# A list scheduler's prices for TensorE operations are replaced in a two-layer transformer block

## The chip, the cores and the metric

The kernel runs on one core of a Trainium2 chip. The metric is the device time of one execution in microseconds, the median of the timed runs.

## The reference

Two layers of a diffusion transformer work on 256 latent tokens and 256 context tokens of width 1024, all in 32-bit floats. In short:

```python
for l in range(2):
    mod_l = silu(c) @ w_ada[l] + b_ada[l]                # six rows: shift, scale, gate, twice
    h = x * (1 + sc1) + sh1                              # the context likewise, with its own rows
    ya, yb, yc, yd = four attentions of one projection h @ w_in[l]
    #   latent, neighbourhood, differential, grouped-query; 4 heads each
    #   latents read latents and context, the context reads context only
    out = (sum_i sigmoid(gate_i) * (y_i @ w_branch[l, i])) @ w_out[l]
    x = layer_norm(ALPHA * x + g1 * out)
    h = x * (1 + sc2) + sh2
    x = layer_norm(ALPHA * x + g2 * (silu(h @ w_gate) * (h @ w_up)) @ w_down[l])
return x                                                 # the latents
```

The context stream stops after the attentions' keys and values of the second layer, so that layer's queries, gates and FFN cover 256 tokens instead of 512.

## The kernel before

Every matrix product is made of three: both operands are split into a high and a low part on the reduced 32-bit grid of TensorE, and high*high, high*low and low*high are added in one PSUM bank (`mm3`). A weight tile of 128x1024 arrives by one DMA of 512 KB into `wr`; ScalarE casts it to the high part `wh`, VectorE subtracts for the low part `wl`. In the first layer most products have a moving operand of 512 columns, in the second of 256. The activations are `hh` and `hl`, those of the FFN `fh` and `fl`; `mm`, `st` and `o` are the PSUM tiles of projections, of scores and transposes, and of attention outputs.

In neighbourhood and grouped-query attention a score is two products (`scores2`, line 865): one over 128 rows and one over 64 rows, `k,q` 128 and `gt,q` or `l,q` or `k,q` 64 in the profile. The 128-row operand holds a head's parts in both halves of the partitions, so `heads2` (line 853) moves them there by DMAs from SBUF to SBUF:

```python
        self.split(a, lo, ps[:, :n], scale)
        self.move(b[64:, :], a[64:, :])
        self.move(b[:64, :], (lo if q else a)[64:, :])
        self.move(a[64:, :], (lo if q else a)[:64, :])     # after both others have read a
```

The order of the instructions is not written by hand. The kernel is recorded on virtual tiles; `record` (line 249) gives each operation a price in microseconds from `price` (line 280), and a list scheduler orders the instructions of each engine. `schedule` (line 313) runs up to ten passes (`PASSES`, line 227). `forward` (line 382) simulates the engines forward in time; an engine takes, among the operations that are ready by then, the one with the smallest priority number:

```python
            lim = t + LOOK[e]                              # LOOK: 0.03 us for TensorE
            op = min((o for o in ready[e] if o.est <= lim), key=lambda o: (o.prio, o.idx))
            op.start = max(t, op.est)
            free[e] = op.start + op.cost
            if e == "sync":                                # a DMA; dge is 0.65 between SBUF tiles
                dge_free = max(op.end, dge_free) + op.dge
                dma_free = max(dge_free + 0.65, dma_free) + op.bytes / 360e3
                op.end = dma_free + 0.95
```

`backward` (line 333) then goes the same way backwards and makes new priorities of the latest starts; the pass with the shortest simulated length is kept. The tables `SEE` and `SEE_OTHER` hold what passes until one engine sees another's result. Which of a tag's buffers a tile gets is decided by the same passes. `emit` issues everything in the order found, each engine runs its own list in that order, and the waits follow from the data. Because every instruction is issued from one place, all rows of the profile name line 535; the tiles tell them apart.

The prices of the other engines: a ScalarE operation 0.05 or 0.09 + 0.833e-3 per element and 0.093 per pointer operand, a VectorE tensor_tensor 0.065 + n / 960, a DMA 0.05 on its queue.

Of the kernel before, what the change touches and what calls it, by code (L numbers as in the profile page):

```python
# [31 lines left out]
# columns of the per-layer column array  # L32
# [8 lines left out]
# ---------------------------------------------------------------------------  # L41
# Order of issue.  The kernel is recorded on virtual tiles; a list scheduler
# over its dependences then orders the instructions of each engine, and Tile
# gets them in that order (it allocates the tiles and adds every wait).
# ---------------------------------------------------------------------------
# [26 lines left out]
class View:  # L72
    """A view of a virtual tile: shape and strides (in elements) and the calls that make it."""
# [61 lines left out]
    def region(self):  # L135
        """Partitions and the runs of elements in them."""
        row = self.tile.row
        p0 = self.off // row
        p1 = p0 + (self.shape[0] - 1) * (1 if self.strides[0] else 0) + 1
        runs, width = [self.off % row], 1  # L140
        for n, st in sorted(zip(self.shape[1:], self.strides[1:]), key=lambda x: x[1]):
            if st <= width or n == 1 or len(runs) * n > 16:
                width += (n - 1) * st
            else:
                runs = [r + i * st for i in range(n) for r in runs]
        return p0, p1, tuple((r, min(r + width, row)) for r in sorted(runs))
# [36 lines left out]
class Slot:  # L183
    """The i-th memory of a tag's tiles; after: the slots of later phases that lie on it."""
# [34 lines left out]
# time until an engine sees what another has written (its own: what it wrote itself), in us  # L219
# [6 lines left out]
# passes of the scheduler, and how far an engine looks ahead for something more urgent, in us  # L226
# [5 lines left out]
class Plan:  # L232
# [47 lines left out]
    def price(self, op, ins, outs):  # L280
        """Time on the engine, in us."""
        eng, kw = op.eng, op.kw
        if eng == "tensor":
            if op.meth == "transpose":
                n = kw["in_"].shape[0]
                return max(64, n) * 2.1 / 2400
            n = max(64, kw["rhs"].free())
            return n / 2400 + 0.0026 if kw["rhs"].dtype == F32R else n * 4 / 2400 + 0.43
# [24 lines left out]
    def schedule(self):  # L313
        """Forward passes, by program order at first, then by the latest starts that the last pass allows."""
        for op in self.ops:
            for p in op.preds:
                p.succs.append(op)
        best = None
        for _ in range(PASSES):
            order = self.forward()  # L320
            if order is None:
                break
            if best is None or self.length < best[0]:
                best = self.length, order, [o.start for o in order], [(t, t.slot.i) for o in order for t in o.tiles]
            self.backward(order)
        self.length, order, starts, places = best
        for t, i in places:
            t.place = i
        for o, t in zip(order, starts):
            o.start = t  # L330
        return order

    def backward(self, order):
        """The same backwards in time: the order of each engine by latest starts."""
# [47 lines left out]
    def forward(self):  # L382
# [12 lines left out]
        # slots of a tag go to its tiles in the order in which the kernel makes them  # L395
# [64 lines left out]
        while done < len(ops):  # L460
# [30 lines left out]
            for tl in op.tiles:  # L491
                if tl.pool.psum:
                    # no two engines at once on a bank
                    for o in tl.users:
                        if o.eng != e:
                            o.est = max(o.est, op.end + SEE[e].get(o.eng, SEE_OTHER[e]))
# [41 lines left out]
class Net:  # L538
# [14 lines left out]
    # ---------------------------------------------------------------- helpers  # L553
# [9 lines left out]
    def w_tile(self, kind, dtype):  # L563
        """Weight tiles go round the slots of the common pool and, in part, of the phase's own."""
# [15 lines left out]
    def load_w(self, src, n, gain=None, dst=None):  # L580
        """Some weights, split; gain: per-partition factors of equal runs of the columns."""
# [22 lines left out]
    def split(self, hi, lo, src, scale=None):  # L604
        """hi + lo == src, both on the 32-bit reduced grid of the tensor engine."""
# [8 lines left out]
    def blk(self, wh, wl, c0, c1, ps=None):  # L614
        """One block of 128 output features, transposed: [features, tokens c0:c1]."""
# [10 lines left out]
    # ------------------------------------------------------------------ setup  # L626
# [15 lines left out]
    def condition(self, pool):  # L642
        """silu of the conditioning vectors, on all partitions."""
# [12 lines left out]
    # -------------------------------------------------------------- modulation  # L656
    def ada_plan(self, items):
        """Modulation columns to compute, (layer, block, streams) each, handed out by ada_step."""
# [19 lines left out]
    def affine(self, l, m_sh, m_sc, s, lnl=None, lnw=0):  # L678
        """Per-feature scale and shift of the next sublayer's input, [128, 8] each."""
# [16 lines left out]
    def first_h(self):  # L696
        """Shift and scale of the first sublayer by the tensor engine, for some features at a time: rows
        [high and low parts of 2, shift | scale], then columns; behind them the first input itself."""
# [64 lines left out]
    def early(self, q):  # L763
        """The weights by which the first blocks take up one part of the features."""
# [23 lines left out]
    def modulate(self, parts, hi, lo, pool, a):  # L788
        """x * G + B for two pieces of 256 columns, split."""
# [11 lines left out]
    def bc_rows(self, l, m, s, scale, pool):  # L801
        """Row m of the modulation as two [128, 512] tiles, the same on all partitions, by way of DRAM."""
# [13 lines left out]
    # ------------------------------------------------------------- projections  # L816
    def proj_b(self, src, w, per, toks, evac, cols=None):
        """[tokens, w] for each token tile; src(kts) gives the weights of some k tiles."""
# [27 lines left out]
    def qk(self, tag, rows=P):  # L846
        """Two tiles over the queries or the keys, in one."""
# [5 lines left out]
    def heads2(self, ps, q, lo, scale=None):  # L853
        """Two heads of 64 rows, for scores in two products: queries [qh; ql] and [ql; qh], or keys [kh; kh]
        twice, with the low parts of the keys left in lo."""
# [31 lines left out]
    def transposed(self, srcs, rows, cols_of):  # L887
        """[rows, tokens] from token-major tiles, in one bank."""
# [5 lines left out]
    # --------------------------------------------------------------- attention  # L894
    def softmax(self, S, n, scale, rs):
        """exp(scale * (S - max)) and its sum, by rows."""
# [26 lines left out]
    def head(self, s, prob, V, vh, yrow, ydst):  # L923
        """Output of one head on one stream: prob(qt) gives [128 queries, keys]."""
# [33 lines left out]
    def pow_cols(self, ss, n, a, b, tag="rms", bufs=8):  # L958
        """(a * ss + b) ** -0.5"""
# [6 lines left out]
    # neighbourhood attention  # L966
    def na_proj(self, l):
# [11 lines left out]
        for b in range(4):  # L979
            if b == 2 and l:  # L980
                # latents first: their gates need no context
# [38 lines left out]
    # latent attention  # L1020
# [111 lines left out]
    def rope_b(self, v, t, nh, dim, C, S):  # L1132
        """In place on v [128 tokens, nh, dim], tables [128, dim]."""
# [14 lines left out]
    # differential attention  # L1148
# [17 lines left out]
    def df_block(self, l, b, t):  # L1166
        """Queries or keys of two heads, rotated and split."""
# [17 lines left out]
    def df_stack(self, i, q, k, last):  # L1185
        """The three products of a score in one: [qh; qh; ql] against [kh; kl; kh]."""
# [26 lines left out]
    def df_attn(self, l, st, lam_init):  # L1213
# [6 lines left out]
        for c in range(2):  # L1220
            for i in range(2):
                h = 2 * c + i
                sq, sk = qk[h]
                for s in self.streams:
                    def prob(qt):
# [8 lines left out]
                        # (lam e2 / s2) s1 - e1: minus s1 times the difference; the norm takes s1 out  # L1234
# [10 lines left out]
        for t in self.qtoks:  # L1245
# [9 lines left out]
            # (ss / 64 + EPS * s1 ** 2) ** -0.5  # L1255
# [18 lines left out]
    # grouped-query attention  # L1274
# [83 lines left out]
    # ------------------------------------------------------------ gated merge  # L1358
# [6 lines left out]
    def fill(self, n):  # L1365
        """Some steps of work that what comes next does not need."""
# [41 lines left out]
    # ----------------------------------------------------- projection, residual  # L1408
# [3 lines left out]
    def f_pair(self, j):  # L1412
        """1024 columns of the FFN's activation tiles, from block j on."""
# [3 lines left out]
    def residual(self, ps, bc, x, t, half, st, c0=0, c1=512):  # L1417
        """x <- alpha * x + mod * ps, some columns of a token tile, and their statistics."""
# [14 lines left out]
    def out_proj(self, l, t, bc, xs):  # L1433
        """One token tile through w_out, the residual and the norm."""
# [14 lines left out]
    def down_proj(self, l, bc, xs, held, apply, after):  # L1449
        """w_down by halves of 512 features; the last pieces with the tokens outside."""  # L1450
# [7 lines left out]
        for half in range(2):  # L1458
            # the last token tile of all ends by quarters
# [31 lines left out]
    def next_h(self, s, x, aff, pool, kps=range(4)):  # L1491
        """From the normalised x: the modulated, transposed and split input of the next sublayer."""
# [12 lines left out]
    def next_ht(self, t, x, aff, pool):  # L1505
        """The same for one token tile of the latents."""
# [11 lines left out]
    def affine_x(self, x, l, w, tile):  # L1518
        """x * g + b of a norm, by halves of the features."""
# [10 lines left out]
    # ------------------------------------------------------------------- layer  # L1530
# [77 lines left out]
    def ffn_lead_both(self, l, xs, pool, bc, aff):  # L1608
        """w_out, norm and the first FFN blocks, latents in front of the context."""
# [14 lines left out]
    def ffn_lead_lat(self, l, xs, pool, bc, aff):  # L1624
        """w_out, norm and the first four FFN blocks by token tiles."""
# [32 lines left out]
    def ffn(self, l, xs, pool, last, bc, aff):  # L1658
# [18 lines left out]
        if not last:  # L1677
            self.aff1 = aff = {s: self.affine(l + 1, 0, 1, s, l, 1) for s in self.streams}

            def after(t):  # L1680
                # the last two k tiles hold weights that the context still needs
# [46 lines left out]
def _ktile(w, n0, n1):  # L1728
    """[L, K, N] columns n0:n1 -> [L, 128, (K/128) * (n1-n0)]"""
# [5 lines left out]
def _blocks(w):  # L1735
    """[L, K, N] -> [L, N/128, 128, K] with row p of block b holding w[k*128+p, b*128:...] for all k"""
# [4 lines left out]
def _layout(i):  # L1741
# [44 lines left out]
    # neighbourhood bias: rpb[h, i - r + 7, j - w + 15] inside the window, NEG outside  # L1786
# [37 lines left out]
```

## Time and profile before

| | us |
|---|---|
| median of 3 timed runs | 1399.94 |
| lowest and highest of them | 1393.2, 1400.98 |
| span of the profiled execution | 1397.5 |
| TensorE busy in it | 1372.5 |
| mean granted clock of TensorE | 0.994 |

The span runs from the first to the last instruction of one profiled execution. The profile gives no time of its own for that execution beside its span; the median of the timed runs is 2.4 us above the span. Busy time of TensorE counts matmuls whose ends are modelled and which overlap their successors, so the distance between two starts tells the pace of a stretch, and idle time tells where it stood.

### The profile page before, as it was taken

The page shows a single profiled execution, that of the slowest core. Times are in us where ns is not written, and L with a number is a line of the kernel's source. Part 1 is how long each engine was busy: PE and PEld are TensorE (multiplying, and loading weights), DVE is VectorE, ACT ScalarE, POOL GpSimd, SP SyncE. Part 2 cuts the span into 40 slices and gives each one's busy share as a digit, 9 for nine tenths or more (in the row PEclk, how much of TensorE's full clock was granted, in tenths as well). Part 3 has the DMA queues.
Part 4 walks back from the last instruction along what each step waited for, and adds up shares of the span by engine and source line. Part 5 has one row for each costly group of instructions (what it writes and reads, how often), then busy time and mean ns, then how long its engine had stood idle before and what let it go on. Part 6 is the DMA issues. An engine that isn't in the chain of part 4 may idle for free.

```text
span 1397.5 us, 20697 instructions
## 1 busy us (share of the span) xinstructions
PE 1372.5 (98%) x7804; PEld 1180.4 (84%) x7804; DVE 998.8 (71%) x1772; ACT 652.3 (47%) x1163; POOL 59.3 (4%) x111
## 2 busy tenths in 40 slices
PE   7999999999999999999999999999999999999997
PEld 4878988888777889888888888889999889899986
DVE  6667799997685768677655463758879778855554
ACT  6656566743555512223232212356857476544440
POOL 0000100032000000000000000100100200000000
PEclk9999999999999999999999999999999999999999
DMA  8842434345445624566666664264344548566660
GB/s 314 263 122 83 142 108 138 105 131 149 111 131 176 210 77 136 166 184 204 202 197 193 213 194 149 78 188 137 116 134 142 161 141 283 184 204 184 192 181 30
DMA packets 73939, 225.41 MB, mean 161 GB/s; under 512 B 9920, under 2 KB 14448, under 8 KB 73840
## 3 DMA queue, kind: packets, MB, share of 16 engines
q1 hardware_dynamic: 73840, 224.10, 52.2%
q8 instruction: 61, 1.00, 0.3%
q14 instruction: 38, 0.31, 0.1%
HBM read 212.76 MB, written 1.07 MB: 153 GB/s over the span
## 4 chain that ended last, share of the span: by engine, by line
PE 94%; DMA 2%; DVE 1%; ACT 1%; POOL 1%; issue 1%; SPq 0%; POOLq 0%; DVEq 0%; ACTq 0%
PE mm L535 82%; PE st L535 9%; PE o L535 3%; DMA k<-k 1%; ACT wh L535 0%; POOL rms L535 0%; DVE wl L535 0%; DMA wr<-in_w_out 0%; POOL rk L535 0%; DMA wr<-in_w_ada 0%; DVE raw L535 0%; DVE x L535 0%; SPq L535 0%; ACT pth L535 0%; DVE gt L535 0%
## 5 line engine op out<-in xcount | busy, mean ns | idle before, releaser
L535 ACT CAST wh<-wr 128x1024 fp32r<-128x1024 f32 (+2 forms) x261 | 265.8, 1024 | 394.7 <-PE mm L535 323.8
L535 PE MATMUL mm<-hh,wh 128*128 128x512 f32 (+1 forms) x1248 | 424.4, 341 | 1.1 <-ACT wh L535 0.8
L535 PE MATMUL mm<-hh,wl 128*128 128x512 f32 (+1 forms) x1248 | 424.1, 341 | 0.0
L535 PE MATMUL mm<-hl,wh 128*128 128x512 f32 (+1 forms) x1246 | 423.5, 340 | 0.0
L535 DVE TENSOR_TENSOR wl<-wr,wh 128x1024 fp32r<-128x1024 f32 (+3 forms) x260 | 308.6, 1191 | 144.0 <-ACT wh L535 140.5
L535 PEld LDWEIGHTS mm<-hh,wh 128*128 128x128 f32 x1248 | 236.5, 190 | 25.6 <-ACT wh L535 1.6
L535 PEld LDWEIGHTS mm<-hh,wl 128*128 128x128 f32 x1248 | 236.0, 189 | 25.9 <-issue 1.7
L535 PEld LDWEIGHTS mm<-hl,wh 128*128 128x128 f32 x1246 | 236.2, 190 | 24.1 <-issue 0.5
L535 DVE CUSTOM_DVE_ANT_0 y<-wr,silbc 128x1024 bf16<-128x1024 f32 x80 | 96.5, 1221 | 59.3 <-DMA wr<-in_w_ada 59.3
L535 PE MATMUL mm<-wh,hl 128*128 128x256 f32 (+3 forms) x344 | 111.5, 325 | 0.0
L535 PE MATMUL mm<-wl,hh 128*128 128x256 f32 (+3 forms) x344 | 111.4, 324 | 0.0
L535 PE MATMUL mm<-wh,hh 128*128 128x256 f32 (+3 forms) x344 | 111.0, 325 | 0.0
L535 PE MATMUL mm<-wl,fh 128*128 128x512 f32 (+1 forms) x270 | 101.6, 376 | 0.0
L535 PE MATMUL mm<-wh,fl 128*128 128x512 f32 (+1 forms) x270 | 101.6, 376 | 0.0
L535 PE MATMUL mm<-wh,fh 128*128 128x512 f32 (+1 forms) x270 | 101.4, 377 | 0.0
L535 DVE TENSOR_REDUCE s<-st 128x1 f32<-128x512 f32 (+1 forms) x120 | 70.8, 597 | 23.5 <-PE st L535 22.1
L535 ACT ACTIVATE P<-st,s 128x512 f32<-128x512 f32 (+1 forms) x96 | 59.0, 617 | 28.9 <-DVE s L535 27.8
L535 PEld LDWEIGHTS mm<-wh,hl 128*128 128x128 f32 x344 | 65.6, 191 | 5.3 <-issue 1.4
L535 PE MATMUL mm<-y,wh 128*128 128x512 f32 (+1 forms) x256 | 69.4, 346 | 0.3 <-ACT wh L535 0.2
L535 PEld LDWEIGHTS mm<-wl,hh 128*128 128x128 f32 x344 | 65.7, 191 | 4.4 <-issue 0.7
L535 PEld LDWEIGHTS mm<-wh,hh 128*128 128x128 f32 x344 | 65.4, 191 | 4.7 <-DVE y L535 0.4
L535 DVE TENSOR_TENSOR ptl<-st,pth 128x512 fp32r<-128x512 f32 (+1 forms) x96 | 56.7, 596 | 10.0 <-ACT pth L535 9.3
(272 smaller groups left out, 2010.3 us busy)
## 6 DMA issues: line engine op xcount, KB each, us to landing
wr<-in_w_ada SPq DMA_DIRECT2D x87, 512.0 KB, 3.8
wr<-in_w_gu SPq DMA_DIRECT2D x80, 512.0 KB, 4.3
wr<-in_wa SPq DMA_DIRECT2D x74, 512.0 KB, 3.8
wr<-in_w_dn SPq DMA_DIRECT2D x44, 512.0 KB, 4.0
wr<-in_w_br SPq DMA_DIRECT2D x16, 512.0 KB, 3.8
wr<-in_w_out SPq DMA_DIRECT2D x16, 512.0 KB, 3.9
wr<-in_w_gq SPq DMA_DIRECT2D x8, 512.0 KB, 3.6
bc<-in_lnrows SPq DMA_DIRECT2D x16, 256.0 KB, 3.6
```

The source lines that it names most:

```text
L535: o.ins = getattr(getattr(nc, o.eng), o.meth)(*args, **kw)
```

## The change

In `price`, the branch for TensorE gets other numbers. A transpose cost its input's partitions (at least 64) * 2.1 / 2400; now it is 0.108 us, or 0.09 us with at most 32 partitions. A matmul with a reduced-grid operand cost n / 2400 + 0.0026 with n its moving columns (at least 64); now n is at least 256 and the constant is 0.0134 us, or 0.2 us where the product covers at most 64 rows. The branch for plain 32-bit operands goes, which no matmul here took. The other hunks of the diff delete comments and docstrings. Operations, operands and buffers are the same; the scheduler's order, and which buffer of a tag a tile gets, are worked out anew with these prices.

```diff
     def price(self, op, ins, outs):
-        """Time on the engine, in us."""
+
         eng, kw = op.eng, op.kw
         if eng == "tensor":
             if op.meth == "transpose":
-                n = kw["in_"].shape[0]
-                return max(64, n) * 2.1 / 2400
-            n = max(64, kw["rhs"].free())
-            return n / 2400 + 0.0026 if kw["rhs"].dtype == F32R else n * 4 / 2400 + 0.43
+                return 0.108 if kw["in_"].shape[0] > 32 else 0.09
+            n = max(256, kw["rhs"].free())
+            return n / 2400 + (0.0134 if kw["rhs"].shape[0] > 64 else 0.2)
         n = max([v.free() for v in outs + ins] or [1])
```

## Rows read from the trace of the kernel before

**Rows 1.** The page's first part: busy us, share of the span, instructions.

```profile
PE 1372.5 (98%) x7804; PEld 1180.4 (84%) x7804; DVE 998.8 (71%) x1772; ACT 652.3 (47%) x1163; POOL 59.3 (4%) x111
```

**Rows 2.** Stretches: us, busy of each engine (instructions), TensorE clock, DMA share, GB/s.

```profile
700.00:800.00 100.00, 100.00 (x440) 82.05 (x440) 52.87 (x67) 27.48 (x35) 0.00 (x0) 1.00 0.66 201
1230.00:1320.00 90.00, 90.00 (x759) 90.00 (x758) 50.97 (x64) 41.83 (x64) 0.00 (x0) 1.00 0.61 183
75.30:81.40 6.10, 6.10 (x19) 4.35 (x20) 2.66 (x5) 2.43 (x4) 0.00 (x0) 0.50 0.25 68
1119.20:1122.50 3.30, 3.30 (x18) 3.30 (x17) 2.17 (x5) 2.81 (x7) 0.00 (x0) 0.50 0.97 341
0.00:6.25 6.25, 0.00 (x0) 0.00 (x0) 0.18 (x1) 2.75 (x4) 0.74 (x7) 1.00 0.66 202
1389.60:1397.50 7.90, 0.00 (x0) 0.00 (x0) 4.33 (x8) 0.00 (x0) 1.68 (x2) 0.67 0.28 107
```

**Rows 3.** Waits of TensorE's matmuls: us in total, times, longest.

```profile
PE st L535 <- issue: 2.9, 1, 2.9
PE st L535 <- DMA k<-k: 2.4, 2, 1.4
PE mm L535 <- DVE wl L535: 1.3, 1, 1.3
...
PE mm L535 <- ACT wh L535: 1.0, 4, 0.4
PE mm L535 <- ACT raw L535: 0.6, 1, 0.6
PE o L535 <- ACT wh L535: 0.5, 1, 0.5
PE mm L535 <- DVE gt L535: 0.4, 2, 0.2
```

**Rows 4.** Timeline of TensorE at three waits: start, length, instruction [idle before <-releaser].

```profile
75.26 0.77 PE L535 MATMUL st<-k,q 128*128 128x512 f32 x1 [2.92 <-issue]
...
360.79 0.67 PE L535 MATMUL st<-k,q 128*128 128x256 f32 x2 [1.42 <-DMA k<-k]
...
1116.31 2.60 PE L535 MATMUL st<-k,q 128*128 128x512 f32 x6 [0.98 <-DMA k<-k]
```

**Rows 5.** Timeline of the DMA queue: issues of the keys' moves before these waits.

```profile
62.96 1.10 SPq L535 DMA_DIRECT2D k<-k  x2
...
70.44 0.47 SPq L535 DMA_DIRECT2D k<-k  x1
...
351.79 1.23 SPq L535 DMA_DIRECT2D k<-k  x2
...
1105.66 1.14 SPq L535 DMA_DIRECT2D k<-k  x2
```

**Rows 6.** The chain that ended last, at the second and third wait: start, length.

```profile
352.42 3.71 DMA k<-k
...
356.21 4.49 DMA k<-k
...
1106.21 4.97 DMA k<-k
...
1111.26 4.91 DMA k<-k
```

**Rows 7.** Timeline of TensorE around one product of 64 rows.

```profile
116.44 0.39 PE L535 MATMUL st<-k,q 128*128 128x512 f32 x1
116.76 0.50 PE L535 MATMUL st<-gt,q 64*128 64x512 f32 x1
117.19 0.45 PE L535 MATMUL mm<-wh,hl 128*128 128x384 f32 x1
```

**Rows 8.** Instructions by tile and form: count, busy us, mean ns, idle before.

```profile
L535 ACT CAST wh<-wr 128x1024 fp32r<-128x1024 f32 x238 | 248.5, 1049 | 381.8 <-PE mm L535 313.4 <-issue 47.3 <-DMA wr<-in_wa 11.2
...
L535 DVE TENSOR_TENSOR wl<-wr,wh 128x1024 fp32r<-128x1024 f32 x238 | 289.6, 1221 | 131.6 <-ACT wh L535 128.2 <-DMA wr<-in_w_gu 0.2
```

## The prediction

> **What bounds the kernel now.** I read four views in this order. First the busy times: TensorE is busy 98% of the span, VectorE 71%, ScalarE 47% [rows 1]. A busy TensorE need not be at its best pace, so next come stretches in which it never stood. Between 700 and 800 us 440 products, nearly all of 512 columns, start in 100 us: 227 ns from start to start. Between 1230 and 1320 us 759 products of 256 columns start in 90 us: 118.6 ns [rows 2]. Both stretches hold unbroken work at full clock while VectorE is about half idle. The reader is to see that in such a stretch no order of the same products changes anything.
>
> So the time is the 7804 TensorE instructions at their own pace, plus the places where TensorE stands. It stands for 1397.5 - 1372.5 = 25.0 us. The first 6.25 us and the last 7.9 us of the span make 14.2 of these [rows 2]: there the first weights arrive, and there the last normalisation and its output follow the last product. Some 10.8 us are left inside, and the waits name most of them: 2.9 + 2.4 us before score products, and 1.3 + 1.0 + 0.6 + 0.5 + 0.4 = 3.8 us before products that wait for split weights or values [rows 3]. The two waits of the first kind that cost most are followed by a second loss: TensorE is granted half its clock (1.2 instead of 2.4 GHz) for 6.1 us behind the first and for 3.3 us behind the third [rows 2, 4]. Work done at half pace loses half its time, so that is 4.7 us more. All that an order could still win inside the span is therefore about 5.3 + 4.7 + 3.8 = 13.8 us, 1.0%.
>
> **The change part by part.** Nothing is removed or added on the chip: the sum of the work stays, term zero. What moves is the order. The new order can't be read from a profile, so I cost what the prices do to the plan's sense of time.
>
> *Price against row.* A 512-column product was priced at 512 / 2400 + 0.0026 = 215.9 ns and is now 226.7; the row says 227. One of 256 columns was 109.3 and is now 120.1; the row says 118.6. The old plan thus took TensorE for 5% (512) or 8% (256) faster than it is; the new one is right within about 1%. Of the 64-row products one shows 0.43 us to its successor's start, where the new price says 512 / 2400 + 0.2 = 0.413 and the old said 0.216. It also slows its neighbours: the 128-row product of 512 columns ahead of it takes 0.32 us to the next start instead of 0.227 [rows 2, 7]. An order that put two 64-row products side by side might save part of that, but neither price asks for it: zero, with 0.1 us per product as the bound in either direction.
>
> The Trainium skill, in "TensorE: Matmul & The Clock Gate", section "Wait — 56ns, not 53.3ns?", gives a warm back-to-back product N / 2.4 GHz plus about 2.5 ns, 215.7 ns for N = 512. That is the old price, and it speaks against the change. The trace of this kernel disagrees with it by 11 ns a product. Were the page right here, the new plan would think its TensorE work longer than it is, and the loss worked out next would be about twice as large.
>
> *What a dearer product does.* The scheduler takes an operation as soon as it is ready in simulated time and first in priority. While a transfer is under way, it fills the time with other products. The dearer these are, the fewer it puts there. The three waits before scores are of that kind. The keys of two heads are moved in two steps one behind the other, since the third move overwrites what the first two read (issued at 62.96 and at 70.44 us for the first wait [rows 5]). The plan counts for one move of 128 KB 0.65 + 0.65 + 0.36 + 0.95 = 2.6 us; the chain shows 3.71 and 4.49, then 4.97 and 4.91 us [rows 6]. These moves' prices are not changed. Under the old prices the products issued from the first move to the wait lasted 75.26 - 2.92 - 62.96 = 9.4, then 360.79 - 1.42 - 351.79 = 7.6, then 1116.31 - 0.98 - 1105.66 = 9.7 us [rows 4, 5]. If the plan meant each to fit exactly, it meant 9.4 * 109.3 / 118.6 = 8.7, 7.6 * 215.9 / 227 = 7.2 and 9.7 * 109.3 / 118.6 = 8.9 us; the new plan would fill just that, and the waits grow by 0.7 + 0.4 + 0.8 = 1.9 us. If the fillers stand there for lack of other work, nothing changes. I take the middle, +0.9 us, and keep 0 to 1.9.
>
> *The small waits.* The 3.8 us before products that wait for weights, gates or casts [rows 3] come from single places where the plan's order and the real times part. A plan whose dominant engine is priced rightly should place some of them better, and will make some new ones. I take half, -1.9 us; bounds 0 and -3.8.
>
> *Start and tail.* The 6.25 us before the first product hang on a DMA and the first split, the 7.9 us behind the last product on VectorE, GpSimd and the output DMA [rows 2]; none of their prices moves. Zero.
>
> Sum: 1397.5 + 0.9 - 1.9 = 1396.5 us of span. The median of the runs shown stands 2.4 us above the profiled span, so 1396.5 + 2.4 = 1398.9 us, which I round to 1399.
>
> **The rivals.**
>
> *Faster: the score waits go.* A plan with a slower TensorE has more products to spare per microsecond of transfer and may start the moves, or hold a block of gate products, so that all three waits are covered. For it: the waits are few and local, and losing them also brings back both stretches at half clock. Against it: the moves stay underpriced by 1 to 2 us each, which is what makes the waits. With all gone, 1399.9 - 5.3 - 4.7 - 3.8 = 1386.1 us; with the score waits alone, 1390.
>
> *Slower: the margin was what kept TensorE fed.* The other engines are underpriced too. A cast of a weight tile is priced 0.09 + 0.853 = 0.943 us and shows 1.049 on ScalarE; the subtraction is priced 1.132 and shows 1.221 on VectorE [rows 8]. Together they come 0.19 us later than planned. As long as TensorE was underpriced by 5 to 8% as well, the errors cancelled; with TensorE right, a first product of a fresh weight tile can be placed up to 0.19 us too early. The two rows count 238 such tiles. Against it: there is much other work between most splits and their first product, and only some six products now wait for a split, for 2.8 us in all [rows 3]. The mechanism decides once some 37 tiles are hit (37 * 0.19 = 7 us). With 50 of them, 1399.9 + 9.5 = 1409.4 us.
>
> *Nothing much moves.* Old and new prices differ by nearly one factor over most products; the priorities keep their order where all TensorE work is stretched alike. Then the new order differs in detail, the waits stay and the time is that of before, 1399.9 us. The second wait (1.42 us) might also gain a half-clock stretch behind it as the others have: half of 3.3 to 6.1 us, 1402 to 1403.
>
> **How the numbers follow.** Half a per cent, 7 us, is about what a measurement of this kernel can tell from no change; the three runs shown lie 7.8 us apart. The first sum and "nothing much moves" are one case, within that bound: chance 0.49, with a range of its own from 1394 to 1405. The faster rival gets 0.30: its whole reach is 13.8 us, and it needs half of that. The slower rival gets 0.21: it has no ceiling, but TensorE stands so seldom now that it needs many new waits. The predicted time is that of the likeliest, 1399. For the range I go from 1385, just below the time at which every inner wait is gone, to 1410, just beyond the slower rival with 50 tiles; about one in ten is left out at each end.
>
> **What would show it.** Right: the count of TensorE instructions and the pace in unbroken stretches (227 and 119 ns) are as before; the two ends of the span stay at about 6 and 8 us; score products still wait for the keys' moves, each for one to four microseconds, at about the same three places. The faster rival shows as TensorE idle time inside the span falling from 10.8 to below 5 us, and full clock throughout. The slower one shows as many short waits for `wh`, `wl` or softmax results, tens of them at 0.1 to 0.3 us. The forecast is wrong in kind if the pace itself changes, for example if 64-row products or transposes come to stand elsewhere and the products around them start faster or slower with no wait shown; or if a buffer's new place makes a weight load late by a whole transfer at a phase's start.

## The result and the profile after

The changed kernel takes 1411.97 us (median of 4 runs, 1409.97 to 1413.59), the kernel before 1400.46 us beside it. The ratio on record is 1.0099, 95% interval 1.007 to 1.0129 (the two medians alone give 1.0082): slower by 1%, where 1399 us was forecast and 1410 was the upper end of the range. The profiled span is 1410.7 us, 13.2 us longer than before.

The work is as expected the same. Part 1 of the page:

```profile
PE 1379.3 (98%) x7804; PEld 1179.6 (84%) x7804; DVE 998.9 (71%) x1772; ACT 650.0 (46%) x1163; POOL 61.7 (4%) x111
```

Stretches of the changed kernel, columns as in [rows 2]: two without a wait, the two at half clock, and both ends of the span.

```profile
710.00:810.00 100.00, 100.00 (x440) 81.93 (x439) 53.01 (x69) 26.62 (x34) 0.00 (x0) 1.00 0.64 201
1243.00:1333.00 90.00, 90.00 (x759) 90.00 (x758) 51.21 (x64) 41.56 (x63) 0.00 (x0) 1.00 0.57 182
363.90:370.70 6.80, 6.80 (x17) 4.62 (x17) 4.28 (x10) 2.35 (x5) 0.00 (x0) 0.50 0.05 18
1125.20:1131.90 6.70, 6.48 (x18) 4.28 (x18) 3.08 (x7) 4.33 (x8) 0.00 (x0) 0.50 0.87 286
0.00:6.00 6.00, 0.00 (x0) 0.00 (x0) 0.18 (x1) 2.75 (x4) 0.74 (x7) 1.00 0.67 198
1402.80:1410.70 7.90, 0.01 (x1) 0.00 (x0) 4.34 (x8) 0.00 (x0) 1.68 (x2) 0.64 0.29 110
```

The same 440 products in 100 us and 759 in 90 us as in [rows 2], the same 6 and 7.9 us at the ends: the pace and the ends did not move. What moved is in between. TensorE is idle for 1410.7 - 1379.3 = 31.4 instead of 25.0 us, and its busy time is 6.8 us longer for the same 7804 instructions. The two half-clock stretches, 13.5 instead of 9.4 us long in these rows, explain 2 us of that. Part of the rest comes from the waits too: a product counts as busy for its whole 0.39 us where no successor overlaps it, instead of the 0.227 us from start to start. Counted from start to start, against the median of each form in the kernel before, some 8 to 9 of the 13 us lie at the waits, 1 in the products right behind them, 2 in the half clock and 2 around transposes.

The half clock is not what makes most of the loss. The mean granted clock differs from run to run of one kernel. The changed kernel's one run with the highest, 0.998, spans 1408.2 us; the runs of the kernel before with a clock of 0.998 span 1393.2 to 1395.5 us.

The waits of TensorE's matmuls in the changed kernel:

```profile
PE st L534 <- DMA k<-k: 5.1, 2, 2.6
PE mm L534 <- DVE qr L534: 3.1, 5, 0.9
PE mm L534 <- DVE wl L534: 1.8, 4, 0.5
PE mm L534 <- ACT wh L534: 1.6, 4, 0.7
PE st L534 <- DVE ptl L534: 1.3, 2, 0.9
PE mm L534 <- ACT raw L534: 1.2, 3, 0.7
PE mm L534 <- DVE gt L534: 0.9, 1, 0.9
PE st L534 <- DVE qr L534: 0.6, 1, 0.6
PE o L534 <- ACT pth L534: 0.4, 1, 0.4
PE st L534 <- ACT y L534: 0.3, 1, 0.3
PE st L534 <- DVE x L534: 0.3, 1, 0.3
PE o L534 <- DVE hh L534: 0.2, 1, 0.2
```

Those of the kernel before that [rows 3] leave out, besides the first product's:

```profile
PE st L535 <- DVE ptl L535: 1.0, 2, 0.9
...
PE st L535 <- ACT y L535: 0.3, 1, 0.3
PE mm L535 <- DVE qr L535: 0.2, 1, 0.2
```

Against [rows 3]: the waits before scores are 5.1 instead of 5.3 us, in two places instead of three. The small waits, without `ptl`, `y`, `x` and `hh`, add up to 3.1 + 1.8 + 1.6 + 1.2 + 0.9 + 0.6 + 0.4 = 9.6 instead of 3.8 us. Counted alike, with every one that is listed, they go from 5.3 to 11.7 us. The largest is `qr`, the normalised output of the differential attention, with 3.7 us instead of 0.2. The page's chain that ended last shows the same from another side; first the kernel before, then the changed one:

```profile
PE 94%; DMA 2%; DVE 1%; ACT 1%; POOL 1%; issue 1%; SPq 0%; POOLq 0%; DVEq 0%; ACTq 0%
```

```profile
PE 87%; DVE 5%; ACT 2%; DMA 2%; POOL 2%; issue 1%; SPq 0%; POOLq 0%; DVEq 0%; ACTq 0%
```

The chain that sets the end now passes over VectorE, ScalarE and GpSimd in 9% of the span instead of 3%: products stand behind other engines' results at more places. One such place in the timeline of TensorE:

```profile
308.20 0.39 PE L534 MATMUL mm<-hh,wl 128*128 128x512 f32 x1
309.32 0.44 PE L534 MATMUL mm<-ident,qr 128*128 128x128 f32 x2 [0.73 <-DVE qr L534]
309.52 0.47 PE L534 MATMUL mm<-hh,wh 128*128 128x512 f32 x1
309.83 0.39 PE L534 MATMUL mm<-hl,wh 128*128 128x512 f32 x1
...
311.81 0.44 PE L534 MATMUL mm<-ident,qr 128*128 128x128 f32 x2 [0.90 <-DVE qr L534]
```

Gate products with their operands at hand come right behind the transposes that wait. By the rule of `forward` the plan takes an operation that is ready in its own time, so in the plan the transposes were ready by then. The first product behind the wait also takes 0.31 us to the next start (309.52 to 309.83) instead of 0.227.

The moves of the keys, in the chain by time, and the waits behind them in TensorE's timeline:

```profile
352.99 4.67 DMA k<-k
...
357.73 5.22 DMA k<-k
...
1119.91 5.38 DMA k<-k
```

```profile
363.08 0.90 PE L534 MATMUL st<-k,q 128*128 128x512 f32 x2 [2.58 <-DMA k<-k]
...
1125.42 2.93 PE L534 MATMUL st<-k,q 128*128 128x512 f32 x4 [2.55 <-DMA k<-k]
```

Both are at the grouped-query scores, at the same points as the second and third wait of [rows 4], and 1.2 and 1.6 us longer (2.58 and 2.55 instead of 1.42 and 0.98 us); the first wait of before is gone. Each move shown takes 4.7 to 5.4 us, still against 2.6 in the plan.

### The profile page after: what moved, and what is told of

Its sections match the earlier page's. It is cut to its first block, busy times and chain, and to the rows that moved or that the text cites. A ratio compares the mean times of both kernels' runs of the same rounds, so it can differ in the third digit from the quotient of the medians.

```text
span 1410.7 us, 20693 instructions
## 1 busy us (share of the span) xinstructions
PE 1379.3 (98%) x7804; PEld 1179.6 (84%) x7804; DVE 998.9 (71%) x1772; ACT 650.0 (46%) x1163; POOL 61.7 (4%) x111
## 4 chain that ended last, share of the span: by engine, by line
PE 87%; DVE 5%; ACT 2%; DMA 2%; POOL 2%; issue 1%; SPq 0%; POOLq 0%; DVEq 0%; ACTq 0%
PE mm L534 76%; PE st L534 8%; PE o L534 3%; DVE wl L534 1%; DMA k<-k 1%; POOL rms L534 1%; ACT wh L534 1%; ACT P L534 1%; DVE s L534 1%; DMA wr<-in_w_out 0%; DVE raw L534 0%; DVE x L534 0%; POOL rk L534 0%; DVE ptl L534 0%; DMA wr<-in_wa 0%
```

## The experiments

All kernels have the same operations and buffers; each differs from the kernel before or the changed one only in numbers of the planner, so their times compare orders. The changed price of a product stands as `n / 2400 + 0.0134` below, the old one as `n / 2400 + 0.0026`. Ratios are to the kernel before, run on the same chip; they are those on record, and the quotient of the two medians differs from them by up to 0.2%.

**Which part of the change.** The constant alone, the 64-row price alone, a nudge as a control, and the changed kernel with dearer moves.

```diff
 e1_const    -            return n / 2400 + 0.0026
             +            return n / 2400 + 0.0134
 e2_rows64   +            return n / 2400 + (0.0026 if kw["rhs"].shape[0] > 64 else 0.2)
 e3_nudge    +            return n / 2400 + 0.0030
 e4_moves (on the changed kernel)
             -                op.end = dma_free + 0.95
             +                op.end = dma_free + 0.95 + (2.2 if op.dge > 0.6 else 0.0)
             -                op.prio2 = dma + 1.1
             +                op.prio2 = dma + 1.1 + (2.2 if op.dge > 0.6 else 0.0)
```

> Kernel before with one edit in the planner: the constant of a TensorE product is 0.0134 instead of 0.0026 us; products of 64 rows and transposes keep the old prices. Margin theory (products priced too cheap made the old plan lay more of them in front of every late result; priced right, that cover is gone): nearly the whole loss, 1408 to 1415 us, TensorE idle near 31 us, chain with 5 to 8% on VectorE, ScalarE and GpSimd. Theory of the 64-row price (the surcharge of 0.2 us misplaces the scores): near the time of before, 1397 to 1404. Lottery theory (any other order deals the waits anew, whatever the price): anywhere from 1388 to 1414.

Measured 1416.96 us, ratio 1.0134 (1.0112 to 1.0156). The constant alone carries the whole loss, 2 us above the range of the margin theory. The floor of 256 columns and the prices of the transposes were not tried by themselves.

> Kernel before with one edit in the planner: products over at most 64 rows cost n / 2400 + 0.2 instead of n / 2400 + 0.0026 us; all else keeps the old prices. Margin theory: only 48 products change, the cover of the other waits stays: 1396 to 1404 us. Theory of the 64-row price: 1408 to 1415. Lottery theory: anywhere from 1388 to 1414, so a change of over 5 us in this or in the nudged plan.

Measured 1399.17 us, ratio 1.0 (0.998 to 1.002). With the old prices elsewhere, the 64-row price does nothing; that theory falls.

> Kernel before with the constant of a TensorE product at 0.0030 instead of 0.0026 us, a nudge of 0.4 ns that only breaks ties anew. Margin theory: cover unchanged, the order differs in detail: 1396 to 1404 us. Lottery theory: the nudge scatters as far as the whole change does, over 5 us from before in one direction or the other. Theory of the 64-row price: 1397 to 1404.

Measured 1403.03 us, ratio 1.0031 (1.0011 to 1.0051). Breaking ties anew costs 3 to 4 us: not nothing, but far from the 12 of the change.

> Changed kernel with one more edit in the planner: a move between SBUF tiles lands 2.2 us later in the plan (both passes), so near the 4.7 to 5.4 us that the trace shows instead of 2.6. Margin theory: the two waits before grouped-query scores (5.1 us) and the two stretches at half clock behind them (13.7 us long, 6.8 us lost) go or shrink by more than half, the small waits stay: 1399 to 1405 us. Lottery theory: anywhere from 1388 to 1420. If the moves' waits come from the DMA queue being full rather than from the plan's price, they stay and the time is 1408 to 1415.

Measured 1399.37 us, ratio 1.0004 (0.9988 to 1.002): 12.6 us better than the changed kernel. At a granted clock of 0.998 its runs span 1396.3 to 1398.4 us, against the changed kernel's 1408.2, so 10 us of the gain are not the clock's. In its profile the score waits are down to 0.3 us and the mean granted clock is 0.998, with no half-clock stretch inside the work, while the small waits stay:

```profile
PE mm L534 <- DVE wl L534: 1.9, 4, 1.0
PE mm L534 <- ACT wh L534: 1.8, 3, 0.9
PE st L534 <- ACT P L534: 1.6, 4, 0.7
PE mm L534 <- DVE qr L534: 1.3, 2, 1.1
...
PE st L534 <- DMA k<-k: 0.3, 1, 0.3
```

The score waits shrank by 4.8 us; which waits the rest of the gain comes from is not traced.

**Is it simply cover.** I then held that cheap products lay more work in front of every late result, and that any added margin would pay.

```diff
 e5_oldmoves   (kernel before)  the moves' 2.2 us of e4_moves
 e6_under      (kernel before)  return n / 2400 - 0.0080
 e7_see        (changed kernel)
   -SEE = {... "scalar": {"scalar": 0.1, "tensor": 0.24, ...}, "vector": {"vector": 0.128, "tensor": 0.23, ...
   +SEE = {... "scalar": {"scalar": 0.1, "tensor": 0.64, ...}, "vector": {"vector": 0.128, "tensor": 0.63, ...
 e8_see_moves  (changed kernel)  both
```

> Kernel before (old TensorE prices) with one edit in the planner: a move between SBUF tiles lands 2.2 us later in the plan. Margin theory, in which cheap products cover the small waits and only the moves are too short in the old plan: the three waits before scores (5.3 us) and the stretches at half clock (10.2 us long, 5.1 us lost) go, the small waits stay as before: 1388 to 1394 us. Rival, that every better-placed order is used up by another wait: 1396 to 1402.

Measured 1401.97 us, ratio 1.0014 (0.9996 to 1.0032). A miss: no gain. Score waits still cost 2.2 us, and `qr` alone 3.0 instead of 0.2 us.

> Kernel before with the constant of a TensorE product at -0.0080 instead of 0.0026 us, so every product 10.6 ns cheaper in the plan: a step as long as that of the 0.0134 run, in the other direction. Margin theory: still more products in front of each late result; small waits rarer, the waits for moves shorter: 1388 to 1400 us, and not above before. Rival, that any plan away from the tuned price is worse (the price was tuned to a lucky order): 1405 to 1418, like the step upwards.

Measured 1411.99 us, ratio 1.0079 (1.0054 to 1.0104). A miss: products priced too cheap lose nearly as much as the change does. More cover is not always better.

> Changed kernel with one more edit in the planner: TensorE sees a result of ScalarE or VectorE 0.4 us later than so far (0.64 and 0.63 instead of 0.24 and 0.23). The new product prices stay. Margin theory: the cover that the dearer products took away is given back directly; small waits (about 10 us with their restarts) go for the most part, the two waits for moves with their half clock stay: 1400 to 1406 us. Rival, that the products' prices act through the priorities of all engines and not through the cover: 1408 to 1416, as the changed kernel.

Measured 1415.3 us, ratio 1.0104 (1.0061 to 1.0146). A miss, within the rival's range, and the score waits grew: 8.2 us at three places, with five stretches at half clock, 27 us long together, in a profiled run of 1418.76 us, the longest of four.

> Changed kernel with both edits in the planner: moves land 2.2 us later, and TensorE sees results of ScalarE and VectorE 0.4 us later. Margin theory: both losses go, the gains add up: 1388 to 1395 us, faster than before. Rival, that the gains are not additive because the work that fills one gap is missing at another: 1396 to 1402.

Measured 1403.06 us, ratio 1.0017 (0.9999 to 1.0035): a miss for the margin theory, 1 us above the rival's range. With the moves priced, the later results cost nothing; the gains don't add up. The simple theory of cover falls.

**Level or lottery.** If any new order only deals the waits anew, plans a nudge apart should differ as widely as the change.

```diff
 e9_0022   (kernel before)   return n / 2400 + 0.0022
 e10_0080  (kernel before)   return n / 2400 + 0.0080
 e11_n0138 (changed kernel)  return n / 2400 + (0.0138 if kw["rhs"].shape[0] > 64 else 0.2)
 e12_n0130 (changed kernel)  return n / 2400 + (0.0130 if kw["rhs"].shape[0] > 64 else 0.2)
```

> Kernel before with the constant of a product at 0.0022 instead of 0.0026 us, the nudge of 0.4 ns the other way. Price theory (the time follows the level of the price, best near the old one): as before, 1396 to 1405 us. Lottery theory (each new order deals the waits at the same few places anew; the old plan is one of the good deals): a draw from what the ten plans so far gave, 1398 to 1418, no nearer to before than the others.

Measured 1405.97 us, ratio 1.0042 (1.0026 to 1.0058): 1 us above the range of the price theory.

> Kernel before with the constant of a product at 0.0080 us, half way between 0.0026 and 0.0134. Price theory: between the two, 1404 to 1411 us. Lottery theory: a draw from 1398 to 1418, as likely outside 1404 to 1411 as inside.

Measured 1400.77 us, ratio 1.0007 (0.9997 to 1.0016): below the range of the price theory.

> Changed kernel with the constant at 0.0138 instead of 0.0134 us, a nudge of 0.4 ns around the new price. Price theory: as the changed kernel, 1408 to 1418 us. Lottery theory: a draw from 1398 to 1418, with an even chance of landing 5 us or more below the changed kernel.

Measured 1412.07 us, ratio 1.0087 (1.0067 to 1.0107): as the price theory had it.

> Changed kernel with the constant at 0.0130 instead of 0.0134 us, a nudge of 0.4 ns the other way. Price theory: 1408 to 1418 us. Lottery theory: a draw from 1398 to 1418, with an even chance of landing 5 us or more below the changed kernel.

Measured 1415.56 us, ratio 1.0111 (1.0094 to 1.0128): the same.

Five plans at the new level (the change, 0.0130, 0.0134 without the 64-row price, 0.0138, and the one with late results) lie between 1412 and 1417 us. Five plans from 0.0022 to 0.0080 lie between 1399 and 1406. The lottery is real but 3 to 6 us wide; the level adds some 10 us to it. The one plan half way costs nothing, where a straight line would have put it near 1406; with a draw of 3 to 6 us, a single plan does not rule out a slope.

**The ratio.** The new prices raise TensorE by 5 to 10% against the rest of the plan. One kernel raises everything else as well, one lowers everything else under the old prices.

```diff
 e13_all108 (changed kernel, F = 1.08)    e14_cheap (kernel before, F = 0.926)
 -        op.cost = self.price(op, ins, outs)
 +        op.cost = self.price(op, ins, outs) * (1.0 if eng == "tensor" else F)
 +SEE and SEE_OTHER: every value * F
 -                dge_free = max(op.end, dge_free) + op.dge
 +                dge_free = max(op.end, dge_free) + op.dge * F
 ...               (the DMA's other times in forward and backward likewise)
 e15_moves_pool (changed kernel)  the moves' 2.2 us, and GpSimd 0.45 + n * 2.2e-3, power 0.6 + n * 0.17
 e16_0080_moves (kernel before)   return n / 2400 + 0.0080, and the moves' 2.2 us
```

> Changed kernel with every other time of the planner (prices of ScalarE, VectorE, GpSimd and the DMA queue, the DMA's own times, what passes until an engine sees a result) multiplied by 1.08, about the factor by which the TensorE prices rose. Ratio theory (the cover that a plan lays in front of late results depends on the ratio of prices, and the old one was right by balance): back to 1397 to 1406 us. Rival, that the new TensorE prices by themselves make the worse order: 1408 to 1418.

Measured 1399.98 us, ratio 0.9995 (0.998 to 1.001): the range of the ratio theory.

> Kernel before (old TensorE prices) with every other time of the planner multiplied by 0.926. Ratio theory: the loss without the change, 1408 to 1418 us. Rival: as before, 1397 to 1406.

Measured 1414.71 us, ratio 1.0106 (1.0087 to 1.0126). The ratio theory again. The loss can be made without touching TensorE's prices, and unmade with the new ones in place. The chains that ended last, of e13_all108 and then of e14_cheap:

```profile
PE 91%; DVE 3%; POOL 2%; DMA 1%; ACT 1%; issue 1%; SPq 0%; POOLq 0%; DVEq 0%; ACTq 0%
```

```profile
PE 83%; DVE 8%; DMA 2%; POOL 2%; ACT 2%; issue 2%; SPq 0%; POOLq 0%; DVEq 0%; ACTq 0%
```

The two largest waits of e14_cheap besides the first product's are those of the changed kernel, the keys' moves and `qr`:

```profile
PE st L538 <- DMA k<-k: 5.7, 2, 3.2
PE mm L538 <- DVE qr L538: 2.6, 3, 1.0
```

In e13_all108 the moves' wait shrank, but that for `qr` is as long:

```profile
PE mm L537 <- DVE qr L537: 2.7, 3, 1.3
...
PE st L537 <- DMA k<-k: 1.1, 1, 1.1
```

So `qr` alone doesn't tell a slow plan from a fast one (e5_oldmoves has 3.0 us of it), and neither do the moves: 7.8 us in e9_0022, which takes 1406 us, and 3.0 us in e6_under, which takes 1412. What sorts the plans is all of TensorE's idle time, span less busy time, in the profiles. It is 31.4 to 36.0 us in the seven that take about 1412 us or more, and 23.6 to 30.6 us in the eleven that take 1406 us or less, the kernel before among them; the two groups lie only 0.8 us apart.

> Changed kernel with moves landing 2.2 us later and GpSimd operations priced 0.29 to 0.3 us higher (0.45 + 2.2e-3 n, power 0.6 + 0.17 n), nearer to the 0.2 to 1.2 us of the trace. If the late results that count are those of the moves and of GpSimd's chains: 1388 to 1396 us, better than the moves alone (1399). If only the moves count: 1397 to 1403.

Measured 1400.29 us, ratio 1.0002 (0.9988 to 1.0016). The range of the moves alone: GpSimd's price adds nothing to theirs.

> Product constant at 0.0080 us and moves landing 2.2 us later. If the moves' price is worth about 12 us wherever TensorE is priced above the old level: 1388 to 1394 us. If it only takes back what the new level loses: 1397 to 1404.

Measured 1396.46 us, ratio 0.9971 (0.996 to 0.9983): between the two expectations, and the only plan clearly faster than the kernel before, by 0.3%. Its largest waits besides the first product's:

```profile
PE mm L535 <- ACT raw L535: 2.0, 2, 1.8
PE mm L535 <- ACT wh L535: 1.4, 4, 0.5
...
PE st L535 <- DMA k<-k: 1.0, 2, 0.6
```

As one of sixteen plans, where a nudge alone moves the time by 3 to 6 us, it may owe all or part of its 4 us to the draw.

## Why the prediction was wrong, point by point

*What bounds the kernel* held: same count, same pace, same ends, and most of the difference in waits. One reading was off: the two score waits with a half clock behind them are not the two longest, since 1.42 us without one is more than 0.98 us with one. And the half clock is no more than a small part of the loss: at a granted clock of 0.998 the changed kernel is still 13 to 15 us longer.

*Price against row* held as far as it went: the new prices match the pace, and the 64-row price alone is worth nothing (e2_rows64). That the loss would be about twice as large if the old price were the true pace does not follow: by the same working the first cover would shrink by 9.4 - 9.4 * 109.3 / 120.1 = 0.8 instead of 0.7 us.

*The small waits* is the step that failed. "A plan whose dominant engine is priced rightly should place some of them better": half of 3.8 us was to go, a term of -1.9 with 0 as its upper bound, and they rose by 5.8 to 9.6 us. I took the accuracy of one engine's price for the accuracy of the plan. A list scheduler decides by comparing when TensorE gets through its work with when another engine's result arrives, and the old plan had both too early. The two scaling runs show that the ratio of the prices makes this loss: 1400 us with right TensorE prices and everything else stretched, 1415 us with the old TensorE prices and everything else shrunk. It reaches the time through many waits and no single kind of them.

*What a dearer product does* shows at one place of three. The waits before scores were to grow by 0.9 us; together they fell from 5.3 to 5.1 us, but only because the first one went. At the two grouped-query places they grew by 1.2 and 1.6 us. In the third place the cover shrank from 9.7 to 1125.42 - 2.55 - 1115.44 = 7.4 us, from 79 to 61 products, where I had reckoned with 0.8 us less (the first move is issued at 1115.44 us in the changed kernel). In the second it grew, from 7.6 to 363.08 - 2.58 - 352.36 = 8.1 us and from 30 to 35 products, and the wait is longer because the moves themselves took longer, 4.67 + 5.22 instead of 3.71 + 4.49 us. I had left the half clock out of the sum; it went from 9.4 to 13.5 us in length. That the moves' price can win the loss back at the new level is shown by e4_moves: it alone takes back 12.6 us.

*The slower rival* had the cause, "as long as TensorE was underpriced as well, the errors cancelled", and 1409 us, but the wrong place. Waits for `wl` and `wh` rose by only 0.6 us in all, from 2.8 to 3.4; those for `qr` rose by 3.5 us, those at the two grouped-query places by 2.7. It had 0.21 where it should have led. *Nothing much moves* rested on "all TensorE work is stretched alike"; the stretch is against the other engines, so that was no reason.

What stays open: why pricing products still cheaper loses 12 us (e6_under), and why 0.4 us of margin alone did not help (e7_see). The ratio seems to have a flat best region, and I can't say from these runs where it ends or why. That the small waits come from the ratio and not from the draw is argued from the five plans at one level and the two scaling runs, one plan each, and not shown place by place.

## What to carry to other kernels

Where a planner orders the work, its prices act by their ratio: put the right number into one engine and the balance that hid the other errors can be gone. Here two things took the loss back at the new prices: correcting the price that was farthest off as well (moves of 2.6 us that take 5), or scaling all others together. With the old TensorE prices the corrected moves won nothing (e5_oldmoves). Run a plan with a meaningless nudge beside each, since here the nudge alone is worth up to 6 us.

## What the runs showed of the hardware

GpSimd's small operations stretch when they start while VectorE works on a long one with two inputs in SBUF. From the timeline of the changed kernel, the chain that `qr` waits for:

```profile
306.39 1.22 DVE L534 CUSTOM_DVE_ANT_0 raw<-wr,silbc 128x1024 bf16<-128x1024 f32 x1
...
306.51 1.18 POOL L534 TENSOR_SCALAR rms<-rms 128x4 f32<-128x4 f32 x1
...
307.53 0.69 DVE L534 SCALAR_TENSOR_TENSOR gt<-gt,mm 128x512 f32<-128x512 f32 x1
...
307.78 1.03 POOL L534 TENSOR_TENSOR rms<-rms,mhalf 128x4 f32<-128x4 f32 x1
...
308.84 0.42 DVE L534 TENSOR_TENSOR qr<-st,rms 128x256 f32<-128x256 f32 x1 [0.62 <-POOL rms L534]
309.07 0.22 POOL L534 TENSOR_SCALAR rms<-rms 128x4 f32<-128x4 f32 x1
309.18 1.22 DVE L534 TENSOR_TENSOR wl<-wr,wh 128x1024 fp32r<-128x1024 f32 x1
...
309.37 1.92 POOL L534 TENSOR_TENSOR rms<-rms,mhalf 128x4 f32<-128x4 f32 x1
...
311.33 0.42 DVE L534 TENSOR_TENSOR qr<-st,rms 128x256 f32<-128x256 f32 x1 [0.93 <-POOL rms L534]
```

The same scaling of 4 columns takes 0.22 us, and 1.18 us where a VectorE operation began just before it; the same power takes 1.03 us and 1.92 us. Both VectorE operations (`wr,silbc` and `wr,wh`) read two SBUF tensors, and the long scaling ends 0.08 us behind the first of them: it looks like a wait for its end. The short ones began beside VectorE operations with one input in PSUM (`gt,mm` and `st,rms`). The Trainium skill, in "GPSIMD Engine Reference", section "Specifications", names just that case as one in which GpSimd and VectorE contend for SBUF; the trace agrees, with 0.9 to 1.0 us a time. A list scheduler that prices each engine by itself can't see it.

TensorE was granted half its clock (1.2 GHz) behind idle times of 2.58 and 2.55 us in the changed kernel, and of 2.92 and 0.98 us before [rows 4]: the clock stood at 0.50 for 3.3 to 6.8 us. Behind the 0.98 us it fell only 2.9 us after the wait had ended, at 1119.2 us [rows 2, 4]. After the wait of 1.42 us before it did not fall. So a wait of 1 us can cost 1.7 us more, by an estimate from half of 3.3 us, and the next one nothing. The clock also differs from run to run of one order: 0.993 to 0.998 as the mean granted clock in four runs of the changed kernel, 0.991 to 0.998 in those of the kernel before, with spans of 1403.8 us at 0.991 and 1393.2 to 1395.5 us at 0.998.
